# One residual layer in fp32 on one core: three buffers for rows of v, two parameter loads moved, key and query evictions in separate steps, and PSUM banks kept across two stages

## The chip, the core and the metric

The kernel runs on one core of a Trainium2 chip. The metric is device time in microseconds of one execution, smaller is better. The kernel before takes 1683.75 us (median of 3 runs, 1682.1 to 1683.9). The profile is that of one further execution.

## The reference

One layer with three normalised sub-layers on x, 1024 tokens of width 1024, and 256 memory tokens. Only the first sub-layer (the token mixers) is touched by the change:

```python
h = rms_norm(x, norm_mix_pre[l])
proj = h @ w_in[l]
q, k, v, u, gate_logits = jnp.split(proj, splits, axis=-1)
gate_attn, gate_ssm = jnp.split(jax.nn.sigmoid(gate_logits + b_gate[l]), 2, axis=-1)
o_attn = stick_breaking_attention(q, k, v)
o_ssm = s5_branch(u, ...)
merged = gate_attn * (o_attn @ w_branch_attn[l]) + gate_ssm * (o_ssm @ w_branch_ssm[l])
x = x + rms_norm(merged @ w_out[l], norm_mix_post[l])
...
xa = memory_cross_attention(h, mem_n, xa_wq[l], xa_wk[l], xa_wv[l], xa_wo[l])
...
f = conv_ffn(h, ffn_w_up[l], ffn_conv_w[l], ffn_conv_b[l], ffn_w_down[l])
```

The attention has 8 heads of 64. A score's weight is `sigmoid(z) * prod(1 - sigmoid(z))` over the keys between it and the query, strictly causal. `s5_branch` is a complex diagonal recurrence over 32 groups of 16 channels, then a GELU and a gate `y * sigmoid(y @ w_glu + b_glu)`. q, k, v and u are 512 wide each.

## The kernel before

**Products.** TensorE (PE) multiplies in fp32r. Every fp32 operand is split into a rounded high half and the rest, the low half; a product is three matmuls of 128x128 by 128x512, high by high, high by low and low by high (`mm3`, L146 to L150). One such step needs both halves of both operands, so in front of each matmul there is a cast (mostly on ScalarE, ACT) and then a subtraction (mostly on VectorE, DVE). Eight steps, 24 matmuls, make one 128x512 output in one PSUM bank.

**What sets the order.** Up to L1512 the program is written as events. `at(t, go)` puts a piece of work on a heap with a planned time, `line` puts several behind one another, and `all_events` takes them off in order of time and emits their instructions. For PE, ACT, DVE and POOL (GpSimd) that is the order of the engine's program; the DMAs, which SyncE (SP) issues, come in the same order. A planned time sets the order and nothing else: an engine goes through its own list, waits where an input or a buffer is not there, and all that stands behind on that engine waits as well. A step of PE is planned at `STEP` = 0.70.

**The first stage** (0 to some 60 us) projects x onto v. Eight row tiles of 128 tokens go through `tokens` (n = 0, L419 to L439), 24 matmuls each into one of six `ps_m` banks; then `tokens` with n = 1 does the same for u, with other weights. For each row tile:

- `x_load` (L365) fetches the transposed tile xt (four buffers), `gained` (L409, DVE) multiplies it with the norm's gains, `x_high` (L412, ACT) casts it to the high half of hT and `x_low` (L416, DVE) subtracts for the low half, each in two halves of 4 x 128.
- `rows_load` (L369) fetches the rows as they are, `square` (L389, ACT) sums their squares, and `rate` (L394 on DVE, L395 on POOL) makes 1/rms of it, `rates_x`.
- `put` (L432 to L437) evicts the finished output: ACT multiplies it by the rate into the tile vt (L436), and SP stores vt into v_d in DRAM (L437). vt has one buffer. `put` is planned 8.0 after the tile's last step.

The weights come by `w_load` (L373) and are split by L382 (ACT) and L386 (DVE). The list of loads that stands at time 0.0 ends with two parameters of the recurrence: sbc (L445, 1 MB) and dm (L446, 256 KB, broadcast). sbc is first read by `in_out(0)` (L603, DVE), dm at L614.

**PSUM.** `banks` (L97) opens a pool with some tags, so many banks each, and forgets the tags of the pool around it. The pool `ra` has six banks m and two f; `rb`, the attention's, has two each of z, w, o and f; later pools follow. `ps(tag)` takes the next bank of a tag in turn, and it waits for the readers of that bank's former tile. The tag f is for filling work: outputs of `Job`s (gates, queries and keys, the recurrence's own gate) whose steps are spread between other matmuls. The last user of f in `ra` is the recurrence's gate (`glu_job`), evicted by a sigmoid into og on ACT (L926); the first in `rb` is a filling output for the attention.

**The attention** goes through heads in pairs. `scores` multiplies q by k into z (L992, L993); ACT makes two sigmoids of it (L1003, L1004), DVE a running product (L1008; the order names it SCALAR_TENSOR_TENSOR, the profile TENSOR_TENSOR_SCAN), POOL a product (L1014); `transposes` turns the weights by PE (L1028), ACT and DVE split them into wth (L1035) and wtl (L1040), and `weigh` multiplies by v (L1053).

**Evictions of queries and keys** are `parts` in `qk_job` (L307 to L318), planned at one time t. There are 16 of them: four head pairs, keys and queries, two halves of the 1024 tokens. For a key DVE first multiplies the bank by the row of rates (L309) and SP reloads that row (L286). Then for each of the two lanes (one head each, 64 partitions): ACT casts the high half out of the bank (L314), DVE makes the low half from the bank and that cast (L315), and for keys SP copies both to the other 64 partitions (L317, L318). So the two engines alternate: cast, low half, cast, low half.

Of the kernel before, what the change touches and what calls it, by code (L numbers as in the profile page):

```python
# [11 lines left out]
F32 = mybir.dt.float32  # L12
# [3 lines left out]
ALU = mybir.AluOpType  # L16
# [4 lines left out]
P = 128  # L21
# [24 lines left out]
def kernel(ctx: ExitStack, tc: tile.TileContext, a: dict, out: bass.AP, dbg=None):  # L46
    nc = tc.nc
    V, G, C, T = nc.vector, nc.gpsimd, nc.scalar, nc.tensor
    dma = nc.sync.dma_start
# [33 lines left out]
    bgate = const.tile([P, 16], F32, name="bgate")  # L83
    bglu = const.tile([P, 4], F32, name="bglu")
# [5 lines left out]
    row_k = pr_.tile([P, 512], F32, name="row_k")  # L90
# [4 lines left out]
    psum = {}  # L95

    @contextmanager  # L97
    def banks(**tags):

        outer = dict(psum)  # L100
        with tc.tile_pool(name="ps_" + "_".join(tags), bufs=1, space=PSUM, reuse_waits="tile") as pool:
            psum.clear()
            psum.update({t: (pool, w, n) for t, (w, n) in tags.items()})
            yield
        psum.clear()
        psum.update(outer)

    def ps(tag):
        pool, w, n = psum[tag]
        return pool.tile([P, w], F32, tag=tag, name="ps_" + tag, bufs=n)  # L110
# [20 lines left out]
    def f(ap):  # L131
        return ap.bitcast(F32)
# [14 lines left out]
    def mm3(acc, sh, sl, mh, ml, first, last):  # L147
        T.matmul(acc, sh, mh, start=first, stop=False)  # L148
        T.matmul(acc, sh, ml, start=False, stop=False)  # L149
        T.matmul(acc, sl, mh, start=False, stop=last)  # L150
# [80 lines left out]
    STEP = 0.70  # L231
    events, seen = [], []

    def at(t, go):
        heapq.heappush(events, (t, len(seen), go))
        seen.append(t)
# [12 lines left out]
    class Job:  # L249
# [10 lines left out]
        def high(self, t):  # L260
            self.wh = wpool.tile([P, 1024], F32R, tag="w", name="wh")
            C.copy(self.wh[:, :self.n], self.ws[:, :self.n])

        def low(self, t):
            self.wl = wpool.tile([P, 1024], F32R, tag="w", name="wl")
            V.tensor_tensor(self.wl[:, :self.n], self.ws[:, :self.n], f(self.wh[:, :self.n]), op=ALU.subtract)
# [18 lines left out]
    def rates_load(h):  # L285
        dma(row_k, rx_d[4 * h:4 * h + 4].rearrange("t p -> (t p)").partition_broadcast(P))  # L286
# [15 lines left out]
    def qk_job(pp, key):  # L302
        def out(t, h, sl, acc):
            Q, K, kl = qk[pp]
            hi, scale = (K, 1.0) if key else (Q, 0.125)

            def parts(t):  # L307
                if key:
                    V.tensor_tensor(acc, acc, row_k, op=ALU.mult)  # L309
                    rates_load(1 - h)  # L310
                for i in range(2):
                    ln, xl = slice(64 * i, 64 * i + 64), slice(64 - 64 * i, 128 - 64 * i)
                    lo = kl[i][ln, sl] if key else hi[i][xl, sl]
                    C.mul(hi[i][ln, sl], acc[ln], scale)  # L314
                    V.scalar_tensor_tensor(lo, acc[ln], scale, f(hi[i][ln, sl]), op0=ALU.mult, op1=ALU.subtract)  # L315
                    if key:
                        dma(f(hi[i][xl, sl]), f(hi[i][ln, sl]))  # L317
                        dma(f(kl[i][xl, sl]), f(lo))  # L318

            at(t, parts)  # L320

        def start():

            qk[pp] = [[pqk.tile([P, S], F32R, tag=f"{n}{i}", name=f"{n}{i}") for i in range(2)] for n in ("q", "k", "kl")]

        return Job(a["w_in_T"][4 + pp if key else pp], out, start if key else None)
# [6 lines left out]
    def h_hi(k, sl):  # L333
        return hT[0][k // 4][:, k % 4, sl]

    def h_lo(k, sl):
        return hT[1][k // 4][:, k % 4, sl]

    def g3(ap):
        return ap.rearrange("p (g c) -> p g c", c=16)  # L340

    wx = ExitStack()
    px = wx.enter_context(tc.tile_pool(name="px", bufs=1, side="left"))
    ra = ExitStack()
    ra.enter_context(banks(m=(512, 6), f=(512, 2)))
    pa = ra.enter_context(tc.tile_pool(name="pa", bufs=1, side="right"))
    r0 = ExitStack()
    p0 = r0.enter_context(tc.tile_pool(name="p0", bufs=1, side="right", reuse_waits="tile"))
# [6 lines left out]
    sbc = pq.tile([P, 4, 512], F32, name="sbc")  # L355
    dm = pa.tile([P, 32, 16], F32, name="dm")
# [3 lines left out]
    def x_load(t, kk=None):  # L360

        if t not in xt:
            xt[t] = p0.tile([P, KT, P], F32, tag="xt", name="xt", bufs=4)
        ks = slice(0, KT) if kk is None else slice(4 * kk, 4 * kk + 4)
        dma(xt[t][:, ks], a["x_T"][t].rearrange("p (k t) -> p k t", t=P)[:, ks])  # L365

    def rows_load(t):
        rows_x[t] = p0.tile([P, D], F32, tag="xr", name="xr", bufs=2)
        dma(rows_x[t], a["x"][t * P:(t + 1) * P, :])  # L369
# [50 lines left out]
    def tokens(now, n, i, k):  # L420

        sl = slice(i * P, (i + 1) * P) if n == 0 else slice(i, S, 8)
        if k == 0:
            accs_[n, i] = ps("m")
        acc = accs_[n, i]
        wh, wl = (w[:, (k % 2) * 512:(k % 2 + 1) * 512] for w in pair[n, k // 2])
        mm3(acc, h_hi(k, sl), h_lo(k, sl), wh, wl, k == 0, k == KT - 1)
        if k < KT - 1:
            return

        def put(t):
            if n:  # L432
                C.activation(U[:, :, i, :], g3(acc), AF.Identity, bias=zcol, scale=r8[:, i:i + 1])
                return
            vt = pa.tile([P, 512], F32, tag="vt", name="vt", bufs=1)
            C.activation(vt, acc, AF.Identity, bias=zcol, scale=rates_x[:, 0, i:i + 1])  # L436
            dma(v_d[i * P:(i + 1) * P, :], vt)  # L437

        at(now + STEP + (0.2 if n else 8.0), put)  # L439

    line(0.0, (lambda: x_load(0, 0), 0), (lambda: dma(gcol, a["g_cols"]), 0), (lambda: w_load(0, 0), 0),
         (lambda: x_load(1, 0), 0), (lambda: w_load(0, 1), 0), (lambda: dma(sp, a["ssm_p"]), 0), (lambda: x_load(0, 1), 0),
         (lambda: w_load(0, 2), 0), (lambda: x_load(1, 1), 0), (lambda: w_load(0, 3), 0), (lambda: rows_load(0), 0),
         (lambda: x_load(2), 0), (lambda: rows_load(1), 0), (lambda: x_load(3), 0),
         (lambda: dma(bgate, a["b_gate"]), 0), (lambda: dma(bglu, a["b_glu"]), 0), (lambda: dma(sbc, a["ssm_bc"]), 0),  # L445
         (lambda: dma(dm.rearrange("p g c -> p (g c)"), a["ssm_d"].partition_broadcast(P)), 0))  # L446

    def w_part(n, c, j):

# [348 lines left out]
    for c in range(4):  # L798
        for t in range(2):
            for k in (2 * c, 2 * c + 1):  # L800
                pe(STEP, tokens, 0, t, k)
    for t in range(2, KT):
        last_v = clock
        for k in range(KT):
            pe(STEP, tokens, 0, t, k)
    at(u_begin + 8.0, lambda _: open_t())
    steady = [lambda t, r=r, k=k: tokens(t, 1, r, k) for r in range(8) for k in range(KT)]
    u_begin = clock
    for c in range(4):
# [57 lines left out]
    while timed:  # L867
        t0, _, took, go, n = heapq.heappop(timed)
# [85 lines left out]


    rb = ExitStack()
    rb.enter_context(banks(z=(512, 2), w=(512, 2), o=(512, 2), f=(512, 2)))
    rqk = ExitStack()
    pqk = rqk.enter_context(tc.tile_pool(name="pqk", bufs=2, side="right", reuse_waits="tile"))
    rat = ExitStack()  # L960
# [135 lines left out]
    t, nf, begun, last_z = 0.0, 0, {}, 1e9  # L1096
# [385 lines left out]
    for n, (ch, go, args, last) in enumerate(steady):  # L1482
        while timed and timed[0][0] <= clock + STEP / 2:
            _, _, took, turn_, x = heapq.heappop(timed)
# [16 lines left out]
    while timed:  # L1501
        _, _, took, turn_, x = heapq.heappop(timed)
# [7 lines left out]
    by_time.close()  # L1510
    r5.close()
    rb.close()  # L1512
    mk, mv = mem_kv
    rps = ExitStack()
    rps.enter_context(banks(m=(512, 4), a=(512, 3), t=(512, 1)))

    def xa_q(h, hp):
# [612 lines left out]
    for s in range(last + 1):  # L2130
        prep()
        w, r = 1 + s // 7, s % 7
# [53 lines left out]
    for prod in (2, 1, 5, 6, 3, 7):  # L2186
        acc = bank_b if prod in (2, 5, 3) else bank_a
# [123 lines left out]
```

## Time and profile before

| | |
|---|---|
| median of 3 runs | 1683.75 us (1682.1 to 1683.9) |
| the profiled execution | 1685.56 us, its span 1683.8 us |
| granted TensorE clock over the span | 0.994 |
| HBM read, written | 203.98 MB, 67.38 MB; 161 GB/s over the span |

How to read the rows: L12 is line 12 of the kernel as printed here. `out<-in` are the program's tiles with sizes as partitions x elements. In rows of the timeline the first number is the start in us from the span's start, the second the duration (of the whole run where `x3` says that three such instructions follow one another), and a bracket holds the time that the engine stood idle before it and what it waited for. In rows of the waits stand the total, how many, and the longest. In rows of stretches stand start and end, length, PE's busy time and instructions, granted clock, DMA share and GB/s. SPq is SP's DMA issue. A granted clock of 1.00 is full speed.

### The profile page before, as it was taken

What the parts mean: (1) busy time and instruction counts of PE and PEld (TensorE: products, weight loads), DVE (VectorE), ACT (ScalarE), POOL (GpSimd) and SP (SyncE); (2) the same over time, 40 slices, a digit from 0 to 9 for tenths busy, and PEclk for the clock granted to TensorE, in tenths of its full rate; (3) what the DMA queues carried; (4) which work ended last, traced back from release to release, by engine and by line L of the source; (5) the groups of instructions that cost most, each with busy time, mean ns of one, the idle gap of its engine ahead of it and who ended that gap; (6) DMA issues with size and microseconds to landing.
All of it is one profiled execution on the core that took longest, in us unless ns stands there. A gap on an engine that the chain in (4) does not pass through costs nothing.

```text
span 1683.8 us, 22448 instructions
## 1 busy us (share of the span) xinstructions
PE 1650.1 (98%) x8126; PEld 1383.7 (82%) x8126; DVE 1160.6 (69%) x1608; ACT 879.3 (52%) x1458; POOL 221.1 (13%) x242
## 2 busy tenths in 40 slices
PE   8999999999999999999999999999999999999998
PEld 6998877888788988887888888878888888788886
DVE  6778736766766677556645578878887778865473
ACT  5444345766666554335444456555655556654441
POOL 5000002323332000000120000111111111000010
PEclk9999999999999999999999999999999999999999
DMA  8411143232432964454413575667777676696672
GB/s 316 123 46 62 60 142 92 80 94 65 121 98 91 321 220 141 151 195 160 163 63 113 186 278 178 187 202 203 216 208 200 188 197 186 205 334 234 192 237 84
DMA packets 125438, 279.26 MB, mean 166 GB/s; under 512 B 23696, under 2 KB 28304, under 8 KB 125200
## 3 DMA queue, kind: packets, MB, share of 16 engines
q1 hardware_dynamic: 113664, 251.35, 45.4%
q0 software_dynamic: 9360, 18.09, 6.2%
q10 hardware_dynamic: 2304, 8.39, 1.3%
q8 instruction: 64, 1.05, 0.3%
q14 instruction: 46, 0.38, 0.1%
HBM read 203.98 MB, written 67.38 MB: 161 GB/s over the span
## 4 chain that ended last, share of the span: by engine, by line
PE 45%; DVE 5%; DMA 2%; ACT 2%; issue 1%; POOL 0%; DVEq 0%; SPq 0%; POOLq 0%; ACTq 0%
PE ps_p L1897 7%; PE ps_p L1895 7%; PE ps_p L1896 7%; PE ps_d L2158 4%; PE ps_d L2159 4%; PE ps_d L2160 4%; PE ps_m L148 1%; PE ps_m L149 1%; PE ps_m L150 1%; PE ps_a L149 1%; DMA wv<-in_ffn_up_T 1%; PE ps_a L150 1%; PE ps_a L148 1%; DMA ws<-in_xa_wo_N 1%; PE ps_p L149 1%
## 5 line engine op out<-in xcount | busy, mean ns | idle before, releaser
L148 PE MATMUL ps_f<-hT,wh 128*128 128x512 f32 x384 | 165.5, 431 | 0.8 <-ACT og L926 0.8
L150 PE MATMUL ps_f<-hT,wl 128*128 128x512 f32 x384 | 150.9, 393 | 0.0
L149 PE MATMUL ps_f<-hT,wh 128*128 128x512 f32 x384 | 150.6, 392 | 0.0
L1895 PE MATMUL ps_p<-qS,bm 128*128 128x512 f32 (+2 forms) x368 | 141.4, 384 | 2.9 <-DVE uu L1913 2.4
L1896 PE MATMUL ps_p<-qS,bm 128*128 128x512 f32 (+2 forms) x368 | 141.2, 384 | 1.7 <-DVE qS L1722 1.7
L154 DVE TENSOR_TENSOR dn<-raw,dn 128x1024 fp32r<-128x1024 f32 x77 | 93.4, 1223 | 69.8 <-ACT dn L153 66.6
L1897 PE MATMUL ps_p<-qS,bm 128*128 128x512 f32 (+2 forms) x368 | 141.4, 384 | 0.0
L1008 DVE TENSOR_TENSOR_SCAN s<-s,zcol 128x128 f32<-128x128 f32 (+3 forms) x96 | 102.2, 1065 | 42.8 <-ACT s L1003 41.8
L153 ACT CAST dn<-raw 128x1024 fp32r<-128x1024 f32 x77 | 80.5, 1054 | 94.3 <-PE ps_d L2160 43.1
L1014 POOL TENSOR_TENSOR s<-s,s 128x127 f32<-128x127 f32 (+4 forms) x96 | 93.9, 981 | 259.0 <-DVE s L1008 231.4
L2158 PE MATMUL ps_d<-dn 128*128 128x512 f32 x308 | 120.6, 392 | 3.0 <-ACT uu L1908 3.0
L2159 PE MATMUL ps_d<-dn 128*128 128x512 f32 x308 | 120.3, 391 | 0.0
L2160 PE MATMUL ps_d<-dn 128*128 128x512 f32 x308 | 120.3, 391 | 0.0
L1897 PE MATMUL ps_p<-qA,bm 128*128 128x512 f32 (+2 forms) x272 | 104.9, 386 | 0.5 <-DVE bm L1828 0.5
L1895 PE MATMUL ps_p<-qA,bm 128*128 128x512 f32 (+2 forms) x272 | 105.1, 386 | 0.0
L1896 PE MATMUL ps_p<-qA,bm 128*128 128x512 f32 (+2 forms) x272 | 105.0, 386 | 0.0
L1840 POOL DMA_DIRECT2D bm<-in_ffn_up_T x61 | 53.3, 874 | 356.7 <-ACT bm L1839 162.7
L1908 ACT COPY uu<-ps_p 128x512 f32<-128x512 f32 (+2 forms) x90 | 51.4, 571 | 82.8 <-PE ps_p L1897 82.8
L150 PEld LDWEIGHTS ps_f<-hT,wl 128*128 128x128 f32 x384 | 72.0, 188 | 16.2
L1895 PEld LDWEIGHTS ps_p<-qS,bm 128*128 128x128 f32 x368 | 69.7, 189 | 17.4 <-ACT bm L1841 2.2
L1003 ACT ACTIVATE s<-ps_z,rates_x 128x128 f32<-128x128 f32 (+3 forms) x96 | 56.5, 589 | 50.4 <-PE ps_z L993 24.4
L1896 PEld LDWEIGHTS ps_p<-qS,bm 128*128 128x128 f32 x368 | 69.8, 190 | 15.2 <-DVE qS L1722 2.0
(546 smaller groups left out, 4465.1 us busy)
## 6 DMA issues: line engine op xcount, KB each, us to landing
raw<-sd SPq DMA_DIRECT2D x77, 256.0 KB, 3.2
bm<-in_ffn_up_T POOLq DMA_DIRECT2D x61, 256.0 KB, 5.5
ws<-in_w_in_T SPq DMA_DIRECT2D x24, 512.0 KB, 3.4
ws<-in_xa_wo_N SPq DMA_DIRECT2D x23, 512.0 KB, 4.3
wv<-in_ffn_up_T SPq DMA_DIRECT2D x22, 512.0 KB, 4.2
wg<-in_ffn_up_T SPq DMA_DIRECT2D x22, 512.0 KB, 4.0
dr<-in_ffn_down SPq DMA_DIRECT2D x22, 512.0 KB, 6.5
td<-st SPq DMA_DIRECT2D x44, 256.0 KB, 6.3
```

What stands on the lines that cost most here:

```text
L148: T.matmul(acc, sh, mh, start=first, stop=False)
L149: T.matmul(acc, sh, ml, start=False, stop=False)
L150: T.matmul(acc, sl, mh, start=False, stop=last)
L154: (lo or V).tensor_tensor(dl, src, f(dh), op=ALU.subtract)
L1008: V.tensor_tensor_scan(s2[:, n0:n1][:, ::-1], s2[:, n0:n1][:, ::-1], zcol.to_broadcast([P, n1 - n0]), 1.0 if diag else s2[:, n1:n1 + 1], o ...
L1014: G.tensor_tensor(s1[:, n0:e], s1[:, n0:e], s2[:, n0 + 1:e + 1], op=ALU.mult)
L1895: T.matmul(acc, bm[:, 0, ks], q[:, 0, k, cs], start=alone and k == 0, stop=False, skip_group_check=True)
L1896: T.matmul(acc, bm[:, 0, ks], q[:, 1, k, cs], start=False, stop=False, skip_group_check=True)
L1897: T.matmul(acc, bm[:, 1, ks], q[:, 0, k, cs], start=False, stop=k == 3, skip_group_check=True)
L2158: T.matmul(acc[i], v[:, 0, 0, sl], v[:, 0, 1], start=first, stop=False, skip_group_check=True)
L2159: T.matmul(acc[i], v[:, 0, 0, sl], v[:, 1, 1], start=False, stop=False, skip_group_check=True)
L2160: T.matmul(acc[i], v[:, 1, 0, sl], v[:, 0, 1], start=False, stop=last, skip_group_check=True)
```

## The change

The kernel after has four edits.

1. *Rows of v.* The tile that `put` fills is now vr in the pool p0, with three buffers in place of vt's one, and `put` is planned 7.0 after the last step in place of 8.0.
2. *Parameter loads.* sbc and dm leave the list at 0.0 and are planned at 37.5 and 41.5.
3. *Evictions of queries and keys.* `parts` is cut into `scaled` (keys only, at t), `high` (both ACT casts, and for keys the copies of the high halves; at t, for keys at t + 0.8) and `low` (both DVE low halves, and for keys their copies; at t + 1.4, for keys at t + 2.2).
4. *Filling banks.* The two f banks get a pool of their own that is open from the first stage to the attention's end. `banks(keep="f", ...)` lets the inner pools keep that tag, so the turn between its two banks goes on from `ra` to `rb`.

```diff
-    def banks(**tags):
+    def banks(keep=(), **tags):
...
-            psum.clear()
+            for t in set(psum) - set(keep):
+                del psum[t]
             psum.update({t: (pool, w, n) for t, (w, n) in tags.items()})
...
-            def parts(t):
-                if key:
-                    V.tensor_tensor(acc, acc, row_k, op=ALU.mult)
-                    rates_load(1 - h)
-                for i in range(2):
-                    ln, xl = slice(64 * i, 64 * i + 64), slice(64 - 64 * i, 128 - 64 * i)
+            lanes = [(slice(64 * i, 64 * i + 64), slice(64 - 64 * i, 128 - 64 * i)) for i in range(2)]
+
+            def scaled(t):
+                V.tensor_tensor(acc, acc, row_k, op=ALU.mult)
+                rates_load(1 - h)
+
+            def high(t):
+                for i, (ln, xl) in enumerate(lanes):
+                    C.mul(hi[i][ln, sl], acc[ln], scale)
+                    if key:
+                        dma(f(hi[i][xl, sl]), f(hi[i][ln, sl]))
+
+            def low(t):
+                for i, (ln, xl) in enumerate(lanes):
                     lo = kl[i][ln, sl] if key else hi[i][xl, sl]
-                    C.mul(hi[i][ln, sl], acc[ln], scale)
                     V.scalar_tensor_tensor(lo, acc[ln], scale, f(hi[i][ln, sl]), op0=ALU.mult, op1=ALU.subtract)
                     if key:
-                        dma(f(hi[i][xl, sl]), f(hi[i][ln, sl]))
                         dma(f(kl[i][xl, sl]), f(lo))
 
-            at(t, parts)
+            if key:
+                at(t, scaled)
+            at(t + (0.8 if key else 0.0), high)
+            at(t + (2.2 if key else 1.4), low)
...
-    ra = ExitStack()
-    ra.enter_context(banks(m=(512, 6), f=(512, 2)))
+    rf, ra = ExitStack(), ExitStack()
+    rf.enter_context(banks(f=(512, 2)))
+    ra.enter_context(banks(keep="f", m=(512, 6)))
...
-            vt = pa.tile([P, 512], F32, tag="vt", name="vt", bufs=1)
+            vt = p0.tile([P, 512], F32, tag="vr", name="vr", bufs=3)
...
-        at(now + STEP + (0.2 if n else 8.0), put)
+        at(now + STEP + (0.2 if n else 7.0), put)
...
-         (lambda: dma(bgate, a["b_gate"]), 0), (lambda: dma(bglu, a["b_glu"]), 0), (lambda: dma(sbc, a["ssm_bc"]), 0),
-         (lambda: dma(dm.rearrange("p g c -> p (g c)"), a["ssm_d"].partition_broadcast(P)), 0))
+         (lambda: dma(bgate, a["b_gate"]), 0), (lambda: dma(bglu, a["b_glu"]), 0))
+    at(37.5, lambda _: dma(sbc, a["ssm_bc"]))
+    at(41.5, lambda _: dma(dm.rearrange("p g c -> p (g c)"), a["ssm_d"].partition_broadcast(P)))
...
-    rb.enter_context(banks(z=(512, 2), w=(512, 2), o=(512, 2), f=(512, 2)))
+    rb.enter_context(banks(keep="f", z=(512, 2), w=(512, 2), o=(512, 2)))
...
     rb.close()
+    rf.close()
```

Four pieces of the engines' lists show what moves; PE's and POOL's lists hold the same instructions in the same order as before. Line numbers of the kernel after are higher by 1 to 13. SP's list in the first stage, before, from the last small parameter on (xr are rows of x, xt transposed tiles, wr weights, v_d the rows of v):

```order
L445 DMA bglu<-in_b_glu 128x4
L445 DMA sbc<-in_ssm_bc 128x2048
L446 DMA dm<-in_ssm_d 128x512
L369 DMA xr<-in_x 128x1024 x2
L365 DMA xt<-in_x_T 128x1024
L369 DMA xr<-in_x 128x1024
L365 DMA xt<-in_x_T 128x1024 x2
L437 DMA v_d<-vt 128x512
L369 DMA xr<-in_x 128x1024
L365 DMA xt<-in_x_T 128x1024
L437 DMA v_d<-vt 128x512
```

The same list after, from the third store of v on:

```order
L448 DMA v_d<-vr 128x512
L380 DMA xr<-in_x 128x1024
L384 DMA wr<-in_w_in_N 128x1024 x2
L448 DMA v_d<-vr 128x512
L457 DMA sbc<-in_ssm_bc 128x2048
L380 DMA xr<-in_x 128x1024
L458 DMA dm<-in_ssm_d 128x512
L448 DMA v_d<-vr 128x512
```

sbc and dm stood ahead of the third row load (the first of the two in a row) and stand now behind the fourth store of v and around the row load that follows it; every load between is one or two places further ahead.

DVE's list at the second head pair's first key eviction, before (s are running products of the attention, kl the low halves of keys, wtl of weights):

```order
L309 TENSOR_TENSOR ps_f<-ps_f,row_k 128x512
L315 SCALAR_TENSOR_TENSOR kl_2351<-ps_f,k_2349 64x512
L315 SCALAR_TENSOR_TENSOR kl_2352<-ps_f,k_2350 64x512
L1008 SCALAR_TENSOR_TENSOR s_2390<-s_2390,zcol 128x512
L1008 SCALAR_TENSOR_TENSOR s_2423<-s_2423,zcol 128x256
L1008 SCALAR_TENSOR_TENSOR s_2423<-s_2423,zcol 128x512
L1040 TENSOR_TENSOR wtl<-ps_w,wth 128x256
```

And after:

```order
L311 TENSOR_TENSOR ps_f<-ps_f,row_k 128x512
L1020 SCALAR_TENSOR_TENSOR s_2393<-s_2393,zcol 128x512
L1020 SCALAR_TENSOR_TENSOR s_2418<-s_2418,zcol 128x256
L323 SCALAR_TENSOR_TENSOR kl_2354<-ps_f,k_2352 64x512
L323 SCALAR_TENSOR_TENSOR kl_2355<-ps_f,k_2353 64x512
L1020 SCALAR_TENSOR_TENSOR s_2418<-s_2418,zcol 128x512
L1052 TENSOR_TENSOR wtl<-ps_w,wth 128x256
```

Two of the three scans that followed the low halves stand ahead of them now.

ACT's list at one of this pair's key evictions, before (oT is an output of the attention, s the sigmoids, wth the high halves of weights):

```order
L1063 COPY oT<-ps_o 128x256
L314 ACTIVATE k_2349<-ps_f 64x512
L314 ACTIVATE k_2350<-ps_f 64x512
L1003 ACTIVATE s_2510<-ps_z,rates_x 128x512
L1004 ACTIVATE s_2509<-ps_z,rates_x 128x512
L1035 CAST wth<-ps_w 128x512
```

And after:

```order
L1075 COPY oT<-ps_o 128x256
L1015 ACTIVATE s_2513<-ps_z,rates_x 128x512
L1016 ACTIVATE s_2512<-ps_z,rates_x 128x512
L316 ACTIVATE k_2352<-ps_f 64x512
L316 ACTIVATE k_2353<-ps_f 64x512
L1047 CAST wth<-ps_w 128x512
```

The two sigmoids that followed the casts stand ahead of them now.

## The prediction

> **What bounds the kernel now.** I read the page first, then the waits of PE, then the two stretches in which they lie. Page, span and PE's busy time:
>
> ```profile
> span 1683.8 us, 22448 instructions
> ...
> PE 1650.1 (98%) x8126; PEld 1383.7 (82%) x8126; DVE 1160.6 (69%) x1608; ACT 879.3 (52%) x1458; POOL 221.1 (13%) x242
> ```
>
> PE is busy for 98% of the span and the change neither adds nor removes a matmul. So only two things can move: PE's 33.7 us of idle time (1683.8 - 1650.1), and matmuls that run at a lower granted clock. The longest of PE's waits in the first stage, and all of its waits between 240 and 460 us (line, whom it waits for, us, times, longest):
>
> ```profile
> PE ps_m L148 <- ACT hT L412: 2.9, 1, 2.9
> ```
>
> ```profile
> PE ps_z L992 <- ACT s L1004: 1.9, 3, 1.0
> PE ps_w L1028 <- DVE wtl L1040: 1.5, 2, 1.3
> PE ps_o L1053 <- DVE wtl L1040: 1.4, 2, 0.7
> PE ps_f L148 <- ACT og L926: 0.8, 1, 0.8
> ```
>
> These 8.5 us are what the change can reach; the other 25 us lie where its instructions don't run. Cut at the borders of the projection's row tiles (24 matmuls each), the first stage reads (length, PE busy, granted clock, DMA share, GB/s):
>
> ```profile
> 26.05:31.55 5.50, 5.50 (x25) 1.00 0.80 277
> 31.55:34.66 3.11, 0.19 (x1) 1.00 0.81 327
> 34.66:42.07 7.41, 7.41 (x25) 0.77 0.94 304
> ```
>
> The fourth tile takes 5.50 us; then PE stands for 3.11 us, and the fifth tile takes 7.41 us for the same 24 matmuls, because the granted clock is 0.77 on average. The gap costs 3.11 + (7.41 - 5.50) = 5.02 us, not the 2.9 that the waits show. What holds it is ACT:
>
> ```profile
> 33.33 0.78 ACT L436 ACTIVATE vt<-ps_m,zcol,rates_x 128x512 f32<-128x512 f32 x1 [6.55 <-DMA v_d<-vt]
> 34.00 0.61 ACT L412 CAST hT<-xt 128x512 fp32r<-128x512 f32 x1
> ```
>
> ```profile
> 25.76 0.34 SPq L437 DMA_DIRECT2D v_d<-vt  x1
> ```
>
> The single vt buffer leaves with a store that is issued at 25.76 and has not read it out before 33.3; the second vt waits 6.55 us, and the cast that PE needs is queued behind it.
>
> **The change part by part.**
>
> *Three buffers.* The second and third rows of v no longer wait for a store; the fourth waits for the first one's. The cast of the fifth tile then waits for its input alone:
>
> ```profile
> 28.04 1.22 DVE L409 TENSOR_TENSOR xt<-xt,gcol 128x1024 f32<-128x1024 f32 x1
> 29.18 0.15 DVE L394 TENSOR_SCALAR rstd<-sums_x 128x1 f32<-128x1 f32 x1
> 34.64 0.69 DVE L416 TENSOR_TENSOR hT<-xt,hT 128x512 fp32r<-128x512 f32 x1 [5.32 <-ACT hT L412]
> ```
>
> Its gain multiply ends at 29.26, the cast (0.61) at 29.9, the low half (0.69) at 30.6, before PE needs it at 31.55. So the 5.02 us go. What is late next is DVE, whose list runs from 34.64 to the first low half of the u weights with hardly a pause:
>
> ```profile
> 57.59 3.49 DVE L386 TENSOR_TENSOR wl<-wr,wh 128x1024 fp32r<-128x1024 f32 x3
> ```
>
> ```profile
> 58.89 0.60 PE L149 MATMUL ps_m<-wl,hT 128*128 128x512 f32 x1
> ```
>
> One of three low halves takes 1.16, so the first is ready at 58.75 and its matmul starts at 58.89 (and reads 0.60 long): that chain has no slack. It takes 58.75 - 34.64 = 24.1 us. In the changed kernel it begins at 29.9, or earlier, since the loads that it follows come sooner, and ends by 54.0; PE wants it at 58.89 - 5.02 = 53.87. I take 0.3 us as lost there, with bounds of 0 and 1.5 (two of the row loads arrive up to one copy late). Start: 5.0 - 0.3 = **4.7 us**, bounds 3.5 and 5.0.
>
> On the clock, the trace has a half-rate stretch after one idle gap of 2.9 us, and none after gaps of 1.3. [...]
>
> *Parameter loads later.* 1.25 MB (sbc, dm) leave SP's list ahead of the row loads of the third and fourth tile and come after the fourth v store. Landing time of the first, its first use, and the casts that stand ahead of the fourth v row on ACT:
>
> ```profile
> sbc<-in_ssm_bc SPq DMA_DIRECT2D x1, 1024.0 KB, 9.2
> ```
>
> ```profile
> 54.86 0.48 DVE L603 TENSOR_SCALAR tx<-sbc,sg 128x512 f32<-128x512 f32 x1
> ```
>
> ```profile
> 41.05 1.15 ACT L412 CAST hT<-xt 128x512 fp32r<-128x512 f32 x2 [2.55 <-DVE xt L409]
> ```
>
> The casts end about 37.2 (42.2 less 5.0), the row's store is issued near 38, sbc right after, and it lands near 47.6 if it again takes 9.2. L603 comes at 54.86 - 5.0 = 49.8. Its new wait thus costs nothing, with 2 us to spare; queued behind it on DVE are the u weights' low halves, which PE would wait for one to one. That is inside the bound of 1.5 above.
>
> *Filling banks kept.* In before the attention stage opens a new pool, and its first filling output takes the bank of the last gate output, read by the last sigmoid here; the one before had freed the other bank:
>
> ```profile
> 242.96 0.69 ACT L926 ACTIVATE og<-ps_f,bglu 128x512 f32<-128x512 f32 x1 [1.17 <-PE ps_f L150]
> 245.76 0.69 ACT L926 ACTIVATE og<-ps_f,bglu 128x512 f32<-128x512 f32 x1 [2.12 <-PE ps_f L150]
> ```
>
> ```profile
> 246.50 0.50 PE L148 MATMUL ps_f<-hT,wh 128*128 128x512 f32 x1 [0.78 <-ACT og L926]
> ```
>
> With the ring kept, the next output gets the bank that was free from 243.65 on: **0.8 us**, one answer.
>
> *Three steps.* ACT's and DVE's halves of an eviction alternated, each waiting for the other; the first pair is what L315 (DVE) waited for, the second L314 (ACT):
>
> ```profile
>   ACT q L314: 13.5, 13
>   ACT k L314: 10.5, 16
> ```
>
> ```profile
>   DVE q L315: 6.5, 8
>   DVE kl L315: 6.0, 8
> ```
>
> DVE stood 24.0 us and ACT 12.5 us in these 16 evictions. Now both casts run, then both low halves, and between the steps stand scans and sigmoids that are ready. Two of PE's gaps show how a standing engine became a PE wait. DVE's backlog, and PE behind it:
>
> ```profile
> 279.40 0.69 DVE L315 SCALAR_TENSOR_TENSOR kl<-ps_f,k 64x512 fp32r<-64x512 f32 x1 [0.66 <-ACT k L314]
> 280.12 3.73 DVE L1008 TENSOR_TENSOR_SCAN s<-s,zcol 128x512 f32<-128x512 f32 x3
> 283.89 0.62 DVE L1040 TENSOR_TENSOR wtl<-ps_w,wth 128x256 fp32r<-128x256 f32 x2
> ```
>
> ```profile
> 284.65 0.52 PE L1028 MATMUL ps_w<-ident,s 128*128 128x128 f32 x3 [1.33 <-DVE wtl L1040]
> ```
>
> Two scans now stand ahead of the low halves, where DVE stood 2 x 0.66; the wtl comes at least 1.3 us earlier, and PE's 1.33 go. And ACT, which stood before a key cast with sigmoids behind it:
>
> ```profile
> 292.94 0.59 ACT L314 ACTIVATE k<-ps_f 64x512 fp32r<-64x512 f32 x1 [4.80 <-DVE ps_f L309]
> ```
>
> ```profile
> 296.21 0.39 PE L992 MATMUL ps_z<-k,q 128*128 128x256 f32 x1 [1.00 <-ACT s L1004]
> ```
>
> The two sigmoids are now ahead of the casts, and 1.00 goes. All seven waits of this stretch (1.9 + 1.5 + 1.4 = 4.8 us) lie next to an eviction. The low halves and the copies of their lanes come a scan later (3.73 / 3 = 1.24); the scores of a head pair start tens of us after, except the first pair's. New waits of that kind have no row; I bound them by 0 and 2.0 and take 0.8: **4.0 us**, bounds 2.8 and 4.8 if the old ones go.
>
> [...]
>
> *Sum*: 4.7 + 0.8 + 4.0 = 9.5 us. The profiled execution took 1685.56 us, 1.8 above the median of 1683.75; it would come to 1676.1, and the median to 1683.75 - 9.5 = 1674.25, **1674.3 us**.
>
> **The rivals.** (1) *The attention waits only move.* DVE's work stays as it is and PE next waits for a wtl or a sigmoid elsewhere; for it: removing one wait of a queue often shows the next; against: the standing time really goes. If 0.8 of the 4.8 is won, 4.7 + 0.8 + 0.8 = 6.3: 1677.5 us. (2) *The start fills again*: DVE's chain without slack, or a late sbc, makes a gap as long as the old one in front of the u stage, half clock included. Gain 0.8 + 4.0 = 4.8: 1679.0. (3) *It is handed back*: the three edits work, but a later stage, whose 25 us of waits the change doesn't touch, waits as much longer: about 1683. (4) *Slower*: filling banks come free too late. An eviction now holds its bank through other engines' work. Before:
>
> ```profile
> 252.27 0.70 DVE L309 TENSOR_TENSOR ps_f<-ps_f,row_k 128x512 f32<-128x512 f32 x1 [3.62 <-PE ps_f L150]
> 253.62 0.68 DVE L315 SCALAR_TENSOR_TENSOR kl<-ps_f,k 64x512 fp32r<-64x512 f32 x1 [0.66 <-ACT k L314]
> 254.97 0.69 DVE L315 SCALAR_TENSOR_TENSOR kl<-ps_f,k 64x512 fp32r<-64x512 f32 x1 [0.66 <-ACT k L314]
> ```
>
> From 252.27 to 255.66 it took 3.4 us; the other bank's output takes at least 5.5, so 2.1 are spare. Three scans in the way (3.73) would exceed that by 1.6 on each of 16 outputs: 25.6 lost, 5.5 won, 1703.9. It turns the sign from 0.6 us per output on. Against it: in attention other matmuls stand between a filling output's steps, so an output takes longer than 5.5.
>
> **How the numbers follow.** Forecast 0.62, rivals 0.22, 0.07, 0.05, 0.04. About 0.2% (3.4 us) is what a measurement of this kernel can tell from no change. The forecast and rivals 1 and 2 are faster by more: 0.91; rival 3 is the same: 0.05; rival 4 is slower: 0.04. Low end: the upper bounds, 5.0 + 0.8 + 4.8 = 10.6, give 1673.15, and the shown runs reach 1.65 below their median: 1671.5. High end: rival 2, 1679.0, which takes in rival 1. That leaves out less than 0.2.
>
> **What would show it.** Right: in the changed profile no PE wait on hT near 31.6 and granted clock 1.00 through the fifth tile; the u stage starts near 53.6; no PE wait on og at the stage's turn; the L314 and L315 waits on each other gone, and PE's waits between 235 and 450 below 1 us. Wrong: a gap of over 1 us between 30 and 60, waits of ps_f matmuls on low halves, or PE's idle time after 460 grown by more than 1 us. Below 1671.5 something outside these waits has gained; above 1679.0 one of the three terms is missing.

## The result, and the profile after

The changed kernel takes 1669.39 us (median of 5 runs, 1667.87 to 1671.65), the kernel before 1683.9 in the same series: a ratio of 0.992, with a 95% interval of 0.9908 to 0.9932, so 13.5 us faster, between 11.5 and 15.5. A second series gave 0.9912 (0.9893 to 0.9932). The forecast was 9.5 us and 1674.3, its lower end 1671.5: the sign was right, the gain too small, and the measured time lies below the range.

Span and PE's busy time after, on the page:

```profile
span 1667.6 us, 22460 instructions
...
PE 1644.8 (99%) x8126; PEld 1383.3 (83%) x8126; DVE 1155.3 (69%) x1608; ACT 880.9 (53%) x1458; POOL 216.3 (13%) x242
```

PE's idle time fell from 33.7 to 22.8 us, and its busy time by 5.3, for the same matmuls. The first stage after, cut again at the borders of the fourth and the fifth tile:

```profile
26.21:31.74 5.53, 5.53 (x25) 1.00 0.99 347
31.74:37.27 5.53, 5.53 (x26) 1.00 1.00 392
```

The gap is gone and the fifth tile runs at full clock. The timeline shows why on ACT, and where sbc went on SP:

```profile
24.40 1.44 ACT L447 ACTIVATE vr<-ps_m,zcol,rates_x 128x512 f32<-128x512 f32 x2
25.74 1.05 ACT L400 ACTIVATE xr<-xr 128x1024 f32<-128x1024 f32 x1
26.68 0.19 ACT L400 ACTIVATION_READ_ACCUMULATOR xr<-xr 128x1 f32 x1
28.73 0.62 ACT L423 CAST hT<-xt 128x512 fp32r<-128x512 f32 x1 [1.85 <-DVE xt L420]
```

```profile
38.01 0.44 SPq L457 DMA_DIRECT2D sbc<-in_ssm_bc  x1
```

Two rows of v are evicted one behind the other, and the cast that ran at 34.00 in before now waits for the gain multiply alone. The attention's stretch has one wait of PE left, of all that stood there in before:

```profile
PE ps_w L1040 <- DVE wtl L1052: 0.2, 1, 0.2
```

And DVE's waits for the casts in the evictions, before and after (waits between 235 and 460, and between 235 and 450 us):

```profile
DVE q L315 <- ACT q L314: 12.9, 12, 2.7
DVE kl L315 <- ACT k L314: 10.5, 16, 0.7
```

```profile
DVE q L323 <- ACT q L316: 5.9, 5, 3.3
DVE kl L323 <- ACT k L316: 2.3, 4, 1.3
```

PE's list is the same in both kernels, so the same matmul can be looked up in both, and the difference of its start is what has been won up to there. At the turn to the attention, before and after:

```profile
245.33 0.40 PE L150 MATMUL ps_f<-yh,wl 128*128 128x512 f32 x1
246.50 0.50 PE L148 MATMUL ps_f<-hT,wh 128*128 128x512 f32 x1 [0.78 <-ACT og L926]
246.84 0.40 PE L149 MATMUL ps_f<-hT,wh 128*128 128x512 f32 x1
```

```profile
240.29 0.39 PE L151 MATMUL ps_f<-yh,wl 128*128 128x512 f32 x1
240.52 0.39 PE L149 MATMUL ps_f<-hT,wh 128*128 128x512 f32 x1
240.75 0.40 PE L150 MATMUL ps_f<-hT,wh 128*128 128x512 f32 x1
```

The wait is shown as 0.78. But the matmul behind it started 246.50 - 245.33 = 1.17 us after the one ahead of it, where the same two now stand 0.23 apart, and the next one follows after 0.34 in place of 0.23: the wait cost 0.94 + 0.11 = 1.05 us. In the second rows matmuls overlap: they start every 0.23 us and are recorded as 0.39 long. The idle time of 0.78 starts at the recorded end of the one ahead (245.33 + 0.40), so the 0.16 of overlap that is lost isn't in it, nor are the 0.11 of a slower start.

And a matmul late in the attention, before and after:

```profile
456.02 0.39 PE L148 MATMUL ps_f<-hT,wh 128*128 128x512 f32 x1
```

```profile
443.39 0.39 PE L149 MATMUL ps_f<-hT,wh 128*128 128x512 f32 x1
```

12.63 us are won there, and the span is 16.2 shorter. So 3.6 us more came later, in stages that the change doesn't touch.

### The profile page after: what moved, and what is told of

The parts are those of the page before. It is cut to its first block, busy times and chain, and to the rows that moved or that the text cites. A ratio compares the mean times of both kernels' runs of the same rounds, so it can differ in the third digit from the quotient of the medians.

```text
span 1667.6 us, 22460 instructions
## 1 busy us (share of the span) xinstructions
PE 1644.8 (99%) x8126; PEld 1383.3 (83%) x8126; DVE 1155.3 (69%) x1608; ACT 880.9 (53%) x1458; POOL 216.3 (13%) x242
## 3 DMA queue, kind: packets, MB, share of 16 engines
q8 instruction: 64, 1.05, 0.3%
## 4 chain that ended last, share of the span: by engine, by line
PE 49%; DVE 3%; DMA 2%; ACT 2%; issue 1%; POOL 0%; DVEq 0%; SPq 0%; POOLq 0%; ACTq 0%
PE ps_p L1910 8%; PE ps_p L1908 8%; PE ps_p L1909 8%; PE ps_d L2171 4%; PE ps_d L2172 4%; PE ps_d L2173 4%; PE ps_m L149 1%; PE ps_m L150 1%; PE ps_m L151 1%; PE ps_p L150 1%; PE ps_a L150 1%; PE ps_p L149 1%; PE ps_p L151 1%; PE ps_a L151 1%; PE ps_a L149 1%
## 5 line engine op out<-in xcount | busy, mean ns | idle before, releaser
L1026 POOL TENSOR_TENSOR s<-s,s 128x127 f32<-128x127 f32 (+4 forms) x96 | 89.3, 930 | 256.1 <-DVE s L1020 222.3
L151 PEld LDWEIGHTS ps_f<-hT,wl 128*128 128x128 f32 x384 | 72.1, 188 | 16.2
```

Source lines behind the costliest of these rows:

```text
L1026: G.tensor_tensor(s1[:, n0:e], s1[:, n0:e], s2[:, n0 + 1:e + 1], op=ALU.mult)
```

## The experiments

All gains are against the first profile of before, in us, read from the start of the same matmul: up to the last gate outputs (243.22 in before), across the turn (to 247.07), across the attention (to 456.02), behind it, and of the whole span. The ratio is that of the timed runs.

| kernel | start | turn | attention | behind | span | ratio (95% interval) |
|---|---|---|---|---|---|---|
| changed kernel | 5.03 | 1.05 | 6.54 | 3.55 | 16.2 | 0.992 (0.9908 to 0.9932) |
| changed kernel again | 5.03 | 1.05 | 6.52 | 2.39 | 15.0 | 0.9912 (0.9893 to 0.9932) |
| before again | -0.56 | 0.01 | 0.03 | 1.09 | 0.6 | one run |
| edits 1 and 2 | 5.38 | 0.01 | 0.02 | 3.96 | 9.4 | 0.9975 (0.9966 to 0.9985) |
| edit 1 | 4.90 | 0.01 | 0.01 | 3.85 | 8.8 | 0.9975 (0.9965 to 0.9984) |
| edit 2 | 2.94 | 0.01 | 0.02 | 3.53 | 6.5 | 0.9982 (0.9971 to 0.9992) |
| edit 3 | 0.81 | 0.01 | 6.55 | 3.67 | 11.0 | 0.996 (0.9946 to 0.9974) |
| edit 4 | -1.23 | 1.05 | 0.05 | 2.32 | 2.2 | 0.9999 (0.9988 to 1.001) |
| grouped | 4.47 | 1.05 | 0.16 | 3.36 | 9.1 | 0.9967 (0.9957 to 0.9977) |
| late pairs | 4.46 | 1.05 | -1.50 | 4.68 | 8.7 | 0.9971 (0.996 to 0.9983) |
| key casts early | 4.96 | 1.05 | 4.29 | 1.49 | 11.8 | 0.9924 (0.9907 to 0.9941) |
| low halves early | 5.40 | 1.05 | 2.11 | 4.80 | 13.4 | 0.9938 (0.9922 to 0.9953) |
| wide | 5.31 | 1.05 | 7.13 | 4.41 | 17.9 | 0.9917 (0.9899 to 0.9935) |

The columns of turn and attention repeat to 0.05 us where nothing there was changed. The start runs from -1.23 to 0.81 in the kernels without edits 1 and 2, from 4.46 to 5.40 in those with both, and what lies behind by over 3. With edit 1 most of the start's scatter comes before the fourth tile: from that tile's first matmul (26.05 in before) to the first u matmul (58.66) all nine profiles with three buffers won 4.97 us.

### One edit at a time

*Edits 1 and 2 together* are the kernel before with these lines:

```diff
-            vt = pa.tile([P, 512], F32, tag="vt", name="vt", bufs=1)
+            vt = p0.tile([P, 512], F32, tag="vr", name="vr", bufs=3)
-        at(now + STEP + (0.2 if n else 8.0), put)
+        at(now + STEP + (0.2 if n else 7.0), put)
-         (lambda: dma(bgate, a["b_gate"]), 0), (lambda: dma(bglu, a["b_glu"]), 0), (lambda: dma(sbc, a["ssm_bc"]), 0),
-         (lambda: dma(dm.rearrange("p g c -> p (g c)"), a["ssm_d"].partition_broadcast(P)), 0))
+         (lambda: dma(bgate, a["b_gate"]), 0), (lambda: dma(bglu, a["b_glu"]), 0))
+    at(37.5, lambda _: dma(sbc, a["ssm_bc"]))
+    at(41.5, lambda _: dma(dm.rearrange("p g c -> p (g c)"), a["ssm_d"].partition_broadcast(P)))
```

> The first two edits alone (three buffers for v, sbc and dm later). All: no wait on hT near 31.6, clock 1.00 through the fifth tile, the first u matmul 4.8 to 5.0 us earlier than the 58.7 of before, the attention's waits as before. Theory A (what the late stages gained in the changed kernel, 3.6 us after 460 us, is scatter of one execution against another): the span ends 5 us earlier, give or take 2, the median near 1679. Rival B (the late stages gain of themselves when PE comes earlier): the end gains 5 plus some 3, the median near 1676.

5.38 us were won in the start, 0.02 in the attention, and 3.96 behind it, in the profile: 9.4 in all, more than A's 5 give or take 2, and the median, 1676.83, lies nearer to B's. But before was faster in this series too (1681.66): the timed runs won 4.2 (2.5 to 5.7), which fits A's 5 and not B's 8. The profiled execution of before (1685.56) lies 3.9 above that median. So most of the late gain is that execution's, and not the edits'. "The stages behind" shows where it lost the time, and that 0.85 us of the late gain is these edits' own.

*Edit 1* alone has the first two of these lines.

> Three buffers and the eviction planned 1.0 earlier, sbc and dm left where they were. Theory: the buffers are what takes the gap away, the first u matmul comes 4.5 to 5.0 us earlier and the loads' place is worth under 0.5. Rival D: with 1.25 MB ahead of the third and fourth rows the casts wait for the rows' squares or xt, and 1 us or more of the gap stays.

4.90 won in the start: the buffers are enough, and D falls. The 0.5 that edits 1 and 2 together won more were won ahead of 26.05; from there to the first u matmul both won 4.97. So beside the buffers the loads' place is worth nothing that shows.

*Edit 2* alone has the others.

> The second edit alone (sbc and dm later). Theory: the vt buffer still holds ACT, but the stores have less traffic beside them, so the gap near 31.6 shrinks to 1 to 3 us; the first u matmul comes 0 to 3 us earlier, median 1680 to 1684. Rival E (the loads were what slowed the stores down): the gap goes without the buffers, 4.5 us or more.

2.94 won, near the upper end of what was expected, with vt still single. ACT's second vt in this run:

```profile
29.78 0.78 ACT L436 ACTIVATE vt<-ps_m,zcol,rates_x 128x512 f32<-128x512 f32 x1 [3.56 <-DMA v_d<-vt]
```

The store ahead of it was issued at 25.21 and held vt for 4.6 us, where it was 7.6 in before (25.76 to 33.33), and 7.0 to 8.5 in the four profiles with vt single and the loads in their old place. The store is read out 3.0 us sooner, and PE's wait on hT shrinks from 2.9 to 0.6. What stood right ahead of the store in before was not sbc itself (issued at 11.29) but a row load and two loads of xt, issued at 24.05 and 24.47; here they were issued at 21.05 and 21.47. E asked for 4.5 and falls. Edits 1 and 2 thus do much the same thing: 4.90 and 2.94 apart, 5.03 and 5.38 together.

*Edit 4* alone is the change to `banks` with its three uses.

> The fourth edit alone (filling banks kept). Theory A: the wait on og goes and the matmul at 247.1 comes 1.06 us earlier, 0.78 idle and 0.28 of overlap; nothing else changes before 460; median near 1682.8. Rival C: 0.78 earlier. Rival B (late stages gain of themselves): the end moves by 2 us or more beyond the 1.06.

1.05 at the turn, to 0.01 what the starts of the matmuls had given: A, not C. Its start lost 1.23, since the old gap is still there, was 3.8 us long in this execution, and the half rate around it lasted 6.83 us and not 3.41. The time doesn't tell the edit from nothing (0.9999); only the alignment does. That the median came at 1682.79, where A expected 1682.8, is luck: before took 1681.66 in this series.

*Edit 3* alone replaces `parts` by the three steps.

> The third edit alone (evictions in separate steps). Theory A (a PE wait costs its idle time and also the overlap with the matmul behind it, some 0.27 us each): the matmul that stood at 456.0 comes 5.4 to 6.6 us earlier though the waits that go sum to 4.6, the og wait of 0.8 at the stage's turn stays, median near 1677.5. Rival C (idle time is the whole price): 4.6 earlier, median near 1679.3; what went beyond it in the changed kernel then came from the other edits.

6.55 in the attention, the same as in the changed kernel (6.54 and 6.52): the edits add up, and nothing of the attention's gain came from another edit. The idle time that went there is 4.6 (4.8 less 0.2), so 1.95 more was won. That is A, not C, but not as A had it, with 0.27 on each of the seven waits. Aligned one by one in the changed kernel, five of them (0.38, 1.00, 0.52, 0.70 and 0.72) were worth 0.26 to 0.28 more than their idle time, as at the turn (1.05 - 0.78 = 0.27). The one of 1.33 shrank to 0.24 and was worth the difference, 1.09; the one of 0.15 shrank to 0.09. The other 0.67 was won at three places (287.05, 366.56 and 384.08 in before) at which the profile has 0.06 of idle time in all.

### What in the three steps does it

*Grouped*: both casts, then both low halves, all at the time t.

```diff
-            at(t + (0.8 if key else 0.0), high)
-            at(t + (2.2 if key else 1.4), low)
+            at(t, high)
+            at(t, low)
```

> The changed kernel, but the three steps of an eviction stand at one planned time again (both casts, then both low halves, with nothing placed between them). Theory P (place: what counts is that ready scans and sigmoids stand ahead of the casts and low halves): at most 2 of the attention's 6.5 us are kept, the matmul of 456.0 comes 8 us earlier than in before (start and banks 6.1, plus 2), median near 1675. Rival Q (pairing: what counts is that the engines no longer alternate): 6.5 kept, 12.6 earlier, median as the changed kernel's.

*Late pairs*: written as before, but planned as late as the low halves are.

```diff
-            at(t, parts)
+            at(t + (2.2 if key else 1.4), parts)
```

> The changed kernel with the evictions written as before (cast, low half, cast, low half), the whole of it planned as late as the low halves are in the changed kernel (2.2 for keys, 1.4 for queries). Theory P (place): most of the 6.5 us is kept, 5 or more, as scans and sigmoids stand ahead of the whole eviction. Rival Q (pairing): DVE stands 0.66 twice and ACT once per eviction again, at most 2 kept, median near 1675.

Both theories fall, each by one of the two. Grouping alone keeps 0.16 of 6.5, so Q is wrong; placing the alternating eviction later loses 1.50 against before, so P is wrong. In both PE still waits for wtl, 3.8 and 5.6 us in all, where in before it waited 2.9 for wtl and 1.9 for sigmoids:

```profile
PE ps_w L1040 <- DVE wtl L1052: 2.0, 1, 2.0
PE ps_o L1065 <- DVE wtl L1052: 1.8, 3, 0.7
```

```profile
PE ps_w L1031 <- DVE wtl L1043: 3.5, 2, 2.1
PE ps_o L1056 <- DVE wtl L1043: 2.1, 2, 1.4
```

(Grouped first, then late pairs.) At the longest of them a stretch at half clock of 3.41 us began in each (granted 0.50 from 279.41 to 282.82 in grouped, 0.51 from 293.50 to 296.96 in late pairs), so some 1.7 us of either loss is the clock (3.41 x 0.5), and both theories fall without it too; grouped, before and behind its wait at 279.1:

```profile
276.00:279.41 3.41, 1.43 (x9) 1.00 0.12 28
279.41:282.82 3.41, 3.41 (x12) 0.50 0.00 0
```

What the two have in common is that a step stands directly behind the one that it needs. DVE waited 23.2 us for the casts in grouped and 21.5 in late pairs, against 23.4 in before and 8.2 in the changed kernel. The theory that was left (R): a step must be placed behind the *time* that its input takes on the other engine, with ready work in between, and each engine's share can be won by itself. *Key casts early* puts only the key casts back to t:

```diff
-            at(t + (0.8 if key else 0.0), high)
+            at(t, high)
```

> The changed kernel with the key casts planned at t again, beside the row multiply that they wait for; the low halves stay where the changed kernel has them. Theory R (each step must stand behind the time that its input takes, on either engine; one engine's share can be won alone): ACT stands before key casts again and the three waits on sigmoids return, 1.9 idle and 3 x 0.27, so 3.8 of the attention's 6.5 us are kept. Rival S (nothing is kept unless both engines are free of waits): under 1 kept.

*Low halves early* puts only the low halves back, to where the casts are:

```diff
-            at(t + (2.2 if key else 1.4), low)
+            at(t + (0.8 if key else 0.0), low)
```

> The changed kernel with the low halves planned at the time of the casts (keys t + 0.8, queries t); the key casts stay at t + 0.8. Theory R: DVE stands before each first low half again, the four waits on wtl return, 2.9 idle and 4 x 0.27, the three on sigmoids stay away: 2.7 of 6.5 kept. Rival S: under 1 kept.

4.29 and 2.11 are kept, near the 3.8 and 2.7 of R and far from S. What each loses (2.25 and 4.43) sums to 6.7; grouped lost 6.4, but with the 1.7 of the half-clock stretch that neither of these has. One part of R's expectation didn't come: with the key casts early PE waited not on the sigmoids but on wtl.

```profile
PE ps_w L1040 <- DVE wtl L1052: 2.4, 2, 1.4
```

ACT stood 15.2 us before the key casts in this run, against 9.1 in the changed kernel. How that reached wtl (by way of ACT's casts to wth, or of later sigmoids and scans) wasn't traced.

*Wide* doubles the distances.

```diff
-            at(t + (0.8 if key else 0.0), high)
-            at(t + (2.2 if key else 1.4), low)
+            at(t + (1.6 if key else 0.0), high)
+            at(t + (4.4 if key else 2.8), low)
```

> The changed kernel with twice the planned distances: key casts at t + 1.6, key low halves at t + 4.4, query low halves at t + 2.8. If the distance only has to cover the input (theory R) the 6.5 us stay and the time is that of the changed kernel to within 2 us; DVE's and ACT's remaining waits in the evictions (8.2 and 9.1 us) shrink. Rival T (filling banks come free too late): PE waits on ps_f for low halves, 0.5 us or more on each of some of the 16 outputs, and the median is 1672 or above.

7.13 won in the attention, 0.6 more than the changed kernel, and no wait of PE between 235 and 450 us at all. So no filling bank came free too late, even at twice the distance: T falls. DVE's and ACT's remaining waits in the evictions shrank, as expected, from 8.2 to 4.6 and from 9.1 to 7.5 us. In time wide can't be told from the changed kernel (0.9917 against 0.9912 in the same series).

### The stages behind

> The changed kernel once more. Theory A (late stages scatter by half-clock stretches): up to 460 us as in the first profile to within 1 us, behind it the stretches at half clock differ in number or length; the ratio lies near 1 - 12.6/1684 = 0.9925.

> The kernel before once more, for its profile. Theory A (the 3.6 us that the changed kernel won after 460 us are scatter): up to 460 us the matmuls stand within 1.5 us of the first profile, the difference being the gap at 31.6 and its clock, with the attention's waits of 4.8 the same; behind it the stretches at half clock are others in number or length, and the end differs by 1 to 4 us. Rival B: the same late stages to within 1 us.

Up to 456 us the changed kernel came as it had, to 0.03 us, and before to 0.56, its start. Behind that the first lost 1.2 against its first profile and before won 1.1 against its own. In before the half-clock stretches are others, as A had it: 10.24 us long near 1050, where the first profile has 3.41, and none near 1107. In the changed kernel they are the same ones in both profiles (6.83 us near 1038, 3.41 near 1451), so its 1.2 lies in waits, and that part of A didn't come. The column of the stages behind holds 1.1 to 4.8 for all kernels, and in the main doesn't follow how early they arrive: edit 4 arrives 0.1 later than before and wins 2.3; the changed kernel arrives 12.6 earlier and wins 3.6 or 2.4. So a good part of the 3.6 is that the first profile of before was slow there. One place shows it: PE stood 1.85 us at 1106.57 behind DVE, which waited for a load, where the changed kernel has 0.2 and 0.6, and a half-clock stretch followed that no other profile has. From 1100 to 1116 it took 2.1 to 3.3 us longer than each of the others.

```profile
1103.32 0.69 DVE L1804 TENSOR_TENSOR t<-wv,wg 128x512 f32<-128x512 f32 x1 [2.15 <-DMA wv<-in_ffn_up_T]
```

```profile
1103.59:1107.00 3.41, 1.56 (x7) 1.00 0.74 202
1107.00:1110.41 3.41, 3.41 (x10) 0.50 0.98 279
```

At one place the changed kernel does win time of its own. The same matmul, before and after:

```profile
1375.55 0.47 PE L1895 MATMUL ps_p<-qS,bm 128*128 128x512 f32 x1 [0.59 <-DVE uu L1913]
```

```profile
1359.06 0.39 PE L1908 MATMUL ps_p<-qS,bm 128*128 128x512 f32 x1
```

This wait is 0.59 and 0.48 in the two profiles of before, 0.43 with edit 4 and 0.29 with edit 2. In the ten that reach the matmul of 456 at least 4.0 us earlier it is gone, and each won 0.85 us between 1116 and 1440. Why coming earlier takes it away wasn't traced. The 12.6 and this 0.85 make 13.5; the timed gain is 13.5 in one series (11.5 to 15.5) and 14.8 in the other (11.5 to 18.0).

## Why the prediction was right and wrong

The mechanisms were right, all three, and no rival took their place. What was wrong is the size of one term, the three steps, and to a smaller part that of the filling banks, for one habit: a wait was priced at the idle time that the view of the waits gives.

- *Start*, 4.7 predicted: 5.03 measured, twice; 4.46 to 5.40 in all kernels with edits 1 and 2. The 5.02 came from the lengths of two tiles, from start to start, and so held the whole price, clock included: between the fourth tile and the first u matmul 4.97 went, in each of the nine profiles. The 0.3 taken off for DVE's chain was not lost: the first u matmul, at 58.66 in before, came at 53.85, and at 53.53 in the second profile; 58.66 - 5.02 is 53.64.
- *Loads later*, at nothing: right beside the buffers, and sbc was issued at 38.01 where 38 was expected. It landed 6.4 us later, at 44.4, and was first read at 49.60, so it had 5 us to spare and not 2. But the prediction did not see that these loads were what made the store slow (it held vt for 7.6 us with them ahead, 4.6 without), so that edit 2 alone is worth 2.94: one gap had two causes, and it named one.
- *Filling banks*, 0.8, "one answer": 1.05 measured. The mechanism was exact; the price left out 0.27 of overlap.
- *Three steps*, 4.0 with bounds of 2.8 and 4.8: 6.54 and 6.52 measured, outside both. This is the step that failed, by its size and not its mechanism. Two errors. The upper bound took 4.8 us of idle time as all that could go; edit 3 alone won 6.55, and wide, with no wait left, 7.13. Five waits were worth 1.34 more than their idle time, and 0.67 lay where the profile has next to none. And 0.8 was taken off for new waits, of which none came: the 0.2 that is left is the rest of the old wait of 1.33.
- *The profiled execution*: 12.6 for 9.5 at the attention's end, 2.5 of the 3.1 from the three steps. By itself 12.6 gives 1671.1, just under the range. The rest of the way to 1669.39 lies behind the attention: 0.85 at the wait of 0.59, the remainder in scatter. The prediction's sentence that below 1671.5 something outside these waits has gained is thus true of the smaller part alone.
- *What fills the waits*: that scans and sigmoids stand between the steps is what the gain rests on. Grouped and late pairs bear that out: without filling, 0.16 and -1.50.
- *The signs*: of the L314 and L315 waits on each other only ACT's on the low halves went; DVE still waited 8.2 of 23.4 us for the casts.
- *The rivals*: waits that move (1) came only when the distances were taken out again; the start did not refill (2); nothing was handed back (3). Filling banks too late (4) did not come at twice the distance either. In (4) the limit of 0.6 us per output belongs to the whole gain of 9.5; by the 5.5 that its own sum uses it would be 0.34.
- *The sentence on the clock*, "a half-rate stretch after one idle gap of 2.9 us, and none after gaps of 1.3", was true of the gaps it names, but the same trace has half-rate stretches after waits of 1.52 (until 1050.33) and 1.85 us (until 1106.57). So a wait of that length had a second price here, 1.7 us (3.41 us at 0.50) or more; the last section shows on two executions that its place in time counted.

## What to carry to other kernels

Here a wait of PE between back-to-back matmuls cost some 0.27 us more than its idle time when it went as a whole (1.05 for 0.78 at the turn). So take the distance between the starts of the two matmuls and subtract the usual one, or take two kernels with the same order of matmuls and compare where the same one starts. In a list with a fixed order, put a step behind the time its input takes on the other engine and let ready work stand in between; neither grouping the steps nor moving them together did it (0.16 and -1.50 won, of 6.5). An edit worth 0.06% (1.05 us) showed by alignment where timed runs didn't show it (0.9999, 0.9988 to 1.001).

## What the hardware showed that was not expected

After the same wait of 1.52 us at one place (the first product of the MLP on qS), the clock came back at quite different times. Granted clock in the 10.24 us behind it, in before, the changed kernel and edits 1 and 2:

```profile
1050.33:1060.57 10.24, 10.24 (x50) 0.83 0.42 125
```

```profile
1037.01:1047.25 10.24, 10.24 (x42) 0.67 0.42 126
```

```profile
1043.24:1053.48 10.24, 10.24 (x36) 0.50 0.42 125
```

At half rate for one, two and three parts of 3.41 us (10.24 x 0.17 = 1.7 us lost, 3.4, and 5.1), 50, 42 and 36 matmuls got started. The second profile of before showed the longest there too, so it isn't the change. In the 3.41 us ahead of the third row, PE was busy for 1.90:

```profile
1039.83:1043.24 3.41, 1.90 (x17) 1.00 0.02 5
```

So 1.5 us of standing in 3.41 were enough here for half rate to follow. And a busy part did not always bring the clock back: in the third row PE was busy for all of the 10.24 us and the clock stayed at 0.50.

Up to PE's last matmul, the half-rate stretches of before begin at 7.91, 35.21, 1052.38, 1107.00 and 1465.40 and are 3.41 us long each; in the changed kernel they begin at 1037.86 (6.83 long) and 1450.87 (3.41). In each of the two executions the starts lie whole numbers of parts apart, at 3.413 us a part: 8, 298, 16 and 105 from one to the next in before, 121 in the changed kernel. From 7.91 to 1037.86 it would be 301.7, so the borders of these parts fall elsewhere in the second execution. How a wait lay to them counted in one pair of executions. One matmul waited 2.98 us in before (until 1465.84) and 2.97 in edits 1 and 2 (until 1457.83). In before most of the wait fell into one part, and the next ran at half rate:

```profile
1461.98:1465.40 3.42, 0.88 (x4) 1.00 1.02 359
1465.40:1468.81 3.41, 2.97 (x7) 0.50 0.35 132
```

In the other a border cut the wait in two (1456.27 lies 121.0 parts behind 1043.24, where the half rate of the third row begins), and the clock stayed at 1.00:

```profile
1452.86:1456.27 3.41, 2.00 (x9) 1.00 0.86 294
1456.27:1459.68 3.41, 1.85 (x8) 1.00 0.71 251
1459.68:1463.09 3.41, 3.41 (x17) 1.00 0.01 2
```

Cut at these borders from 20 to 1640 us, in before and the changed kernel every full-rate part with PE busy for 2.05 us or less was followed by half rate (0.55, 0.88, 1.56 and 2.05; 1.51 and 1.89), and none with 2.08 or more was. But in edits 1 and 2 the clock stayed after 2.00 and 1.85, so between 1.85 and 2.05 busy time alone doesn't settle it. The one place with the wait of 1.52 moves the time by up to 3.4 us from run to run, more than the 1.05 of edit 4.
